# The moving matmul operands placed 64 bytes off the stationary ones, modulo 128

## The chip, the core and the metric

The kernel runs on one core of one Trainium2 chip, as one program in one launch. The metric is the device time of that launch in microseconds, as the median of the runs shown. One further execution is profiled; the times of single instructions come from that one.

## What is computed

Two trunk layers of a diffusion backbone on 256 latent tokens of width 2048 (batch 1), with all weights in float32. Cut to what matters:

```python
for i in range(2):                       # layer 0: pooling mixer, layer 1: gated MLP
    shift_x, scale_x, gate_x = split(silu(c) @ ada_w[i] + ada_b[i], 3)
    hx = rms_norm(x, norm_g[i]) * (1 + scale_x) + shift_x
    if i == 0:
        z, g = split(hx @ w_in, 2)       # 2048 -> 2 x 4096
        y = pool_mix(z, w_grp) * scale   # centred window means, then 4 maps 1024 -> 1024
        yx = (y * silu(g)) @ w_out       # 4096 -> 2048
    else:
        z = hx @ w_in                    # 2048 -> 3 x 4096
        u, v = split(gelu(z[:, :8192]), 2)
        v = layer_norm(v, ln_g, ln_b)
        s = w_s . v + b_s                # per 128 positions, 8 head groups
        yx = (u * s * silu(z[:, 8192:])) @ w_out
    x = x + gate_x * yx
```

The context stream of the reference never reaches the output here, and the kernel leaves it out.

## The kernel before

Every large product is `[256 tokens, K] @ [K, 512 columns]`, one block of 512 output columns at a time, for two halves of 128 tokens. One step along K of a block is a unit: 128 rows of K by 512 columns of weight. A float32 product is made of three matmuls in the type float32r (one pass each): both operands are split into a high part and a low rest, and `hi*hi + hi*lo + lo*hi` is summed in PSUM.

In these matmuls the activations are the stationary operand (`lhsT`, 128x128, put into the array by a weight load of its own, which the profile shows as PEld LDWEIGHTS), and the weights are the moving one (`rhs`, 128x512, 2048 bytes in each partition). The stationary tiles are `hh` and `hl` (the normalised input, high and low), `q` (the pooled rows) and `big` (the gated branch before the output product). The moving ones are `whi` and `wlo`. Line 621 multiplies `whi` by the high part, line 622 `wlo` by the high part, line 623 `whi` by the low part. Each matmul has a weight load, since neighbours differ in the stationary operand as recorded.

Weights come from HBM in 1 MB tiles (`raw`, ring of four, queue of SP). Line 98 (ScalarE) copies half a tile into `whi`, rounded to float32r, and line 99 (VectorE) writes the rest into `wlo`, each with three buffers; that is two units. `split_step` runs `LOOK` = 2 such pairs ahead of the matmuls. Between the weights the same ring carries the 96 tiles of `ada_w`, which VectorE multiplies by `silu(c)` and sums (line 245).

Some smaller matmuls use other tiles: line 322 has `big` stationary and the band matrix `bnd` (tag `cst`, 128x256) moving; lines 489 to 491 have the spatial weights (tag `cst`) stationary and `big` or `gs` moving; line 280 transposes through an identity.

SBUF tiles come from pools, and a pool lays its tags one behind the other in the order in which they are first asked for. Pool `sb` (opened first) holds all large tiles, `small` the constants. All sizes in `sb` are multiples of 2048 bytes, and the pool begins at byte 16512 of each partition, which is 129 x 128. So every large tile begins at a multiple of 128.

Of the kernel before, what the change touches and what calls it, by code (L numbers as in the profile page):

```python
# [27 lines left out]
RING = 4  # L28
LOOK = 2
LEAD = (0, 1)  # L30

# [41 lines left out]
def backbone(ctx: ExitStack, tc, x, c, ng, adab, ada, w, pscale, band, invcnt, lng, lnb, wsT, bs, out):  # L75
    nc = tc.nc
    sb = ctx.enter_context(tc.tile_pool(name="sb", bufs=1))
    small = ctx.enter_context(tc.tile_pool(name="small", bufs=1))
    pp = ctx.enter_context(tc.tile_pool(name="pp", bufs=1, space=bass.MemoryType.PSUM))

    uid = [0]

    def st(shape, dt, tag, bufs):
        uid[0] += 1
        return sb.tile(shape, dt, tag=tag, name=f"{tag}_{uid[0]}", bufs=bufs)

    def const(shape, name, dt=F32):
        return small.tile(shape, dt, tag=name, name=name, bufs=1)

    def big(shape, dt):  # L90
        return st(shape, dt, "big", 16)
# [23 lines left out]
    for s, v in enumerate(EARLY):  # L115
        u = sum(e - f for _, f, e in v)
        n1 = 2 * CHUNK[s + 2]
        for j in range(n0, n1):
            while load < begin + u * (j + 1 - n0) / (n1 - n0) / 4 - LEAD[min(s, len(LEAD) - 1)]:
                order.append(("w", load))  # L120
# [22 lines left out]
    def ring_load():  # L143
        e = ring_at[0]
        if e >= len(order):
            return
        ring_at[0] += 1
        kind, i = order[e]
        t = st([P, 2048], F32, "raw", RING)
        src = w[i] if kind == "w" else ada[i]  # L150
        parts = 2 if i < 2 else 1
        for q in range(parts):
            s = slice(q * 2048 // parts, (q + 1) * 2048 // parts)
            nc.sync.dma_start(out=t[:, s], in_=src[:, s])
        ring_tile[e] = t


    c_row = st([P, D], F32, "raw", RING)[0:1, :]
    nc.sync.dma_start(out=c_row, in_=c)
    xin = {}  # L160
# [4 lines left out]
    for _ in range(RING):  # L165
        ring_load()

    ng_sb = const([P, 2, KD], "ng_sb")
    nc.scalar.dma_start(out=ng_sb, in_=ng)
    ab_sb = const([P, 2, 3, KD], "ab_sb")  # L170
    nc.scalar.dma_start(out=ab_sb, in_=adab)
    ident = const([P, P], "ident")
    make_identity(nc, ident)
    ones = const([P, P], "ones")
# [6 lines left out]
    icnt = const([P, NT, NG], "icnt")  # L181
    bs_sb = const([P, 8], "bs_sb")
# [27 lines left out]
    sq0 = const([P, NT, 2], "sq0")  # L210
# [3 lines left out]
    nrm = const([P, 4, NT], "nrm")  # L214
# [191 lines left out]
    sq1 = const([P, NT, 4], "sq1")  # L406
# [194 lines left out]
    for i in range(nsteps):  # L601
# [5 lines left out]
        for u in range(2):  # L607
            n = 2 * i + u
            blk, k = units[n]
            last = n in breaks or k + 1 == blk.nk  # L610
# [109 lines left out]
```

## Time and the profile before

| | |
|---|---|
| three runs | 1403.9, 1407.91, 1408.12 us |
| median | 1407.91 us |
| profiled execution | 1404.94 us, its span from first to last instruction 1403.1 us |
| TensorE busy | 1379.0 us, 98% of the span |
| VectorE busy | 1010.9 us, 72% |
| ScalarE busy | 672.5 us, 48% |
| granted TensorE clock, mean | 0.998 of full |
| HBM | 362.38 MB read, 260 GB/s over the span |

The profiled execution lies 2.97 us below the median and within the range of the three runs. TensorE's busy share counts overlapping matmuls once, so 98% says that the engine had work in flight nearly always. It does not say how fast that work went.

### The profile page before, as it was taken

How to read it: one execution, taken by the hardware profiler on the slowest of the kernel's cores; microseconds unless marked ns; L12 is line 12 of the kernel's file. 1: busy time of each engine (PE TensorE's matmuls, PEld its weight loads, DVE VectorE, ACT ScalarE, POOL GpSimd, SP SyncE). 2: the span in 40 equal slices, each digit the busy share in tenths (PEclk: the TensorE clock that was granted, in tenths of full speed). 3: DMA queues.
4: the chain of work that ended last, by engine and by line, in shares of the span. 5: the costliest groups of instructions: out<-in, count | busy, mean ns of one | idle time of the engine just before them, and what ended most of it. 6: DMA issues, size and time to landing. Idle time of an engine off the chain costs nothing.

```text
span 1403.1 us, 16096 instructions
## 1 busy us (share of the span) xinstructions
PE 1379.0 (98%) x6192; PEld 1136.1 (81%) x6192; DVE 1010.9 (72%) x1305; ACT 672.5 (48%) x792; POOL 0.7 (0%) x6
## 2 busy tenths in 40 slices
PE   6899999999999999999999999999999999999998
PEld 4688887888888888888788888888888888888887
DVE  5899989998998788875765667976665555555553
ACT  8444434554554444444654445545545454544332
POOL 0000000000000000000000000000000000000000
PEclk9999999999999999999999999999999999999999
DMA  8898879878688898896466667776565545556561
GB/s 330 349 337 335 332 295 336 323 300 304 246 325 308 314 352 340 304 347 226 142 264 235 251 222 280 275 257 248 212 243 194 184 180 180 182 186 217 197 214 54
DMA packets 55663, 365.53 MB, mean 261 GB/s; under 512 B 6817, under 2 KB 6817, under 8 KB 13089
## 3 DMA queue, kind: packets, MB, share of 16 engines
q1 hardware_dynamic: 55298, 364.44, 70.2%
q8 instruction: 48, 0.79, 0.2%
q14 instruction: 29, 0.24, 0.0%
q10 hardware_dynamic: 288, 0.07, 0.0%
HBM read 362.38 MB, written 2.10 MB: 260 GB/s over the span
## 4 chain that ended last, share of the span: by engine, by line
PE 91%; DVE 5%; DMA 2%; ACT 1%; issue 1%; SPq 0%; ACTq 0%; DVEq 0%
PE mm L622 29%; PE mm L621 29%; PE mm L623 29%; DVE wlo L99 2%; DVE raw L245 2%; DMA raw<-in_w_dram 1%; PE aux L280 1%; PE aux L322 1%; ACT whi L98 1%; DMA raw<-in_ada_dram 1%; DVE big L628 0%; PE aux L489 0%; PE aux L491 0%; PE aux L490 0%; PE aux L402 0%
## 5 line engine op out<-in xcount | busy, mean ns | idle before, releaser
L99 DVE TENSOR_TENSOR wlo<-raw,whi 128x1024 fp32r<-128x1024 f32 x480 | 585.0, 1223 | 330.3 <-ACT whi L98 328.3
L98 ACT CAST whi<-raw 128x1024 fp32r<-128x1024 f32 x480 | 504.8, 1054 | 655.2 <-PE mm L623 603.1
L621 PE MATMUL mm<-whi,hh 128*128 128x512 f32 x1280 | 497.8, 391 | 4.5 <-ACT whi L98 2.4
L622 PE MATMUL mm<-wlo,hh 128*128 128x512 f32 x1280 | 500.3, 391 | 1.3 <-DVE wlo L99 1.2
L623 PE MATMUL mm<-whi,hl 128*128 128x512 f32 x1280 | 498.7, 390 | 0.0
L621 PEld LDWEIGHTS mm<-whi,hh 128*128 128x128 f32 x1280 | 240.2, 188 | 56.1 <-ACT whi L98 3.9
L622 PEld LDWEIGHTS mm<-wlo,hh 128*128 128x128 f32 x1280 | 240.8, 188 | 53.8 <-DVE wlo L99 4.3
L623 PEld LDWEIGHTS mm<-whi,hl 128*128 128x128 f32 x1280 | 240.7, 188 | 50.1 <-DVE hl L274 0.6
L245 DVE SCALAR_TENSOR_TENSOR raw<-raw,sc 128x1024 f32<-128x1024 f32 x192 | 229.4, 1220 | 17.9 <-DMA raw<-in_ada_dram 17.8
L622 PE MATMUL mm<-wlo,big 128*128 128x512 f32 x512 | 199.3, 389 | 0.0
L623 PE MATMUL mm<-whi,big 128*128 128x512 f32 x512 | 199.2, 389 | 0.0
L621 PE MATMUL mm<-whi,big 128*128 128x512 f32 x512 | 199.2, 389 | 0.0
L622 PEld LDWEIGHTS mm<-wlo,big 128*128 128x128 f32 x512 | 96.1, 188 | 20.3 <-DVE wlo L99 0.4
L623 PEld LDWEIGHTS mm<-whi,big 128*128 128x128 f32 x512 | 96.1, 188 | 19.9
L621 PEld LDWEIGHTS mm<-whi,big 128*128 128x128 f32 x512 | 96.1, 188 | 19.8
L621 PE MATMUL mm<-whi,q 128*128 128x512 f32 x128 | 50.1, 392 | 0.0
L623 PE MATMUL mm<-whi,q 128*128 128x512 f32 x128 | 49.8, 389 | 0.0
L622 PE MATMUL mm<-wlo,q 128*128 128x512 f32 x128 | 49.8, 389 | 0.0
L628 DVE TENSOR_TENSOR big<-mm,big 128x512 f32<-128x512 f32 x52 | 34.0, 684 | 0.4 <-PE mm L623 0.4
L623 PEld LDWEIGHTS mm<-whi,q 128*128 128x128 f32 x128 | 24.0, 188 | 5.0
L622 PEld LDWEIGHTS mm<-wlo,q 128*128 128x128 f32 x128 | 24.0, 188 | 4.9
L621 PEld LDWEIGHTS mm<-whi,q 128*128 128x128 f32 x128 | 24.0, 188 | 4.9
(105 smaller groups left out, 543.7 us busy)
## 6 DMA issues: line engine op xcount, KB each, us to landing
raw<-in_w_dram SPq DMA_DIRECT2D x238, 1024.0 KB, 5.0
raw<-in_ada_dram SPq DMA_DIRECT2D x94, 1024.0 KB, 5.7
big<-in_x_dram SPq DMA_DIRECT2D x4, 512.0 KB, 6.0
raw<-in_ada_dram SPq DMA_DIRECT2D x4, 512.0 KB, 9.0
raw<-in_w_dram SPq DMA_DIRECT2D x4, 512.0 KB, 10.3
q<-in_x_dram SPq DMA_DIRECT2D x8, 256.0 KB, 6.8
gate<-in_lng_dram SPq DMA_DIRECT2D x8, 256.0 KB, 5.0
gate<-in_lnb_dram SPq DMA_DIRECT2D x8, 256.0 KB, 4.3
```

Source lines behind the costliest of these rows:

```text
L98: nc.scalar.copy(hi, src)
L99: nc.vector.tensor_tensor(out=lo, in0=src, in1=hi.bitcast(F32), op=ALU.subtract)
L245: nc.vector.scalar_tensor_tensor(t[:, s], t[:, s], 1.0, sc[:, s], op0=ALU.mult, op1=ALU.mult, accum_out=dots[:, lay, what, k, half:half + 1])
L280: nc.tensor.transpose(tp[:, k - k0, tk * P:(tk + 1) * P], src(k, tk), ident)
L322: nc.tensor.matmul(o, lhsT=z[:, tk, ct * P:(ct + 1) * P], rhs=bnd[:, g, tk, :], start=(n == 0), stop=(n == 3))
L621: nc.tensor.matmul(blk.ps[tk], lhsT=lh, rhs=rh, start=(new and v == u), stop=False)
L622: nc.tensor.matmul(blk.ps[tk], lhsT=lh, rhs=rl, start=False, stop=False)
L623: nc.tensor.matmul(blk.ps[tk], lhsT=ll, rhs=rh, start=False, stop=end)
L628: nc.vector.tensor_tensor(out=blk.part[tk], in0=ps[tk], in1=blk.part[tk], op=ALU.add)
```

## The change

Tiles with the tags `whi`, `wlo` and `cst` come from a pool of their own, `moving`, opened behind `small`. Five small constants go to a fourth pool, `last`, behind it, so that `small` then ends 64 bytes past a multiple of 128.

```diff
+MOVING = ("whi", "wlo", "cst")
+LAST = ("icnt", "bs_sb", "nrm", "sq0", "sq1")
...
     sb = ctx.enter_context(tc.tile_pool(name="sb", bufs=1))
     small = ctx.enter_context(tc.tile_pool(name="small", bufs=1))
+    moving = ctx.enter_context(tc.tile_pool(name="moving", bufs=1))
+    last = ctx.enter_context(tc.tile_pool(name="last", bufs=1))
...
     def st(shape, dt, tag, bufs):
         uid[0] += 1
-        return sb.tile(shape, dt, tag=tag, name=f"{tag}_{uid[0]}", bufs=bufs)
+        pool = moving if tag in MOVING else sb
+        return pool.tile(shape, dt, tag=tag, name=f"{tag}_{uid[0]}", bufs=bufs)
 
     def const(shape, name, dt=F32):
-        return small.tile(shape, dt, tag=name, name=name, bufs=1)
+        pool = last if name in LAST else small
+        return pool.tile(shape, dt, tag=name, name=name, bufs=1)
```

What the two built programs say of the first byte of each tag's first buffer, and of its rest modulo 128 (further buffers follow at 2048, 4096 or 8192 bytes):

```
tag          before: byte, mod 128     changed: byte, mod 128
raw          16512   0                 16512   0
big          49280   0                 49280   0
cst          114816  0                 196416  64
sc           123008  0                 114816  0
hh           131200  0                 123008  0
hl           147584  0                 139392  0
whi          168064  0                 204608  64
wlo          180352  0                 216896  64
q            192640  0                 159872  0
gs, t, gate          0                         0
```

The instructions of every engine, their order and the semaphores that they wait for are the same in both programs, row by row; only addresses and line numbers differ.

## Rows read from the trace of the kernel before

**Rows 1.** The page: span, engines, granted clock, and the chain that ended last.

```profile
span 1403.1 us, 16096 instructions
...
PE 1379.0 (98%) x6192; PEld 1136.1 (81%) x6192; DVE 1010.9 (72%) x1305; ACT 672.5 (48%) x792; POOL 0.7 (0%) x6
...
PE mm L622 29%; PE mm L621 29%; PE mm L623 29%; DVE wlo L99 2%; DVE raw L245 2%; DMA raw<-in_w_dram 1%; PE aux L280 1%; PE aux L322 1%; ACT whi L98 1%; DMA raw<-in_ada_dram 1%; DVE big L628 0%; PE aux L489 0%; PE aux L491 0%; PE aux L490 0%; PE aux L402 0%
```

**Rows 2.** Costliest groups: count | busy us, mean ns | idle before, releaser.

```profile
L99 DVE TENSOR_TENSOR wlo<-raw,whi 128x1024 fp32r<-128x1024 f32 x480 | 585.0, 1223 | 330.3 <-ACT whi L98 328.3
...
L622 PE MATMUL mm<-wlo,hh 128*128 128x512 f32 x1280 | 500.3, 391 | 1.3 <-DVE wlo L99 1.2
...
L622 PE MATMUL mm<-wlo,big 128*128 128x512 f32 x512 | 199.3, 389 | 0.0
...
L622 PE MATMUL mm<-wlo,q 128*128 128x512 f32 x128 | 49.8, 389 | 0.0
L628 DVE TENSOR_TENSOR big<-mm,big 128x512 f32<-128x512 f32 x52 | 34.0, 684 | 0.4 <-PE mm L623 0.4
```

**Rows 3.** Stretches: PE, PEld, DVE, ACT, POOL busy us; clock, DMA share, GB/s.

```profile
45.50:48.30 2.80, 2.80 (x8) 2.19 (x7) 2.80 (x4) 0.11 (x1) 0.00 (x0) 0.50 0.99 410
50.00:200.00 150.00, 148.15 (x657) 120.58 (x656) 134.37 (x192) 68.78 (x79) 0.00 (x0) 1.00 0.87 326
200.00:400.00 200.00, 199.43 (x936) 165.76 (x935) 182.91 (x263) 101.20 (x130) 0.00 (x0) 1.00 0.82 306
400.00:600.00 200.00, 200.00 (x913) 166.27 (x913) 166.58 (x222) 90.75 (x111) 0.00 (x0) 1.00 0.85 323
606.00:645.00 39.00, 39.00 (x174) 32.31 (x173) 29.94 (x43) 18.41 (x22) 0.00 (x0) 1.00 0.82 304
1000.00:1200.00 200.00, 200.00 (x900) 165.89 (x899) 112.80 (x117) 103.20 (x117) 0.00 (x0) 1.00 0.56 199
```

**Rows 4.** Timeline of PE, 606 to 645: start us, us; first and last of 174.

```profile
605.71 0.39 PE L623 MATMUL mm<-whi,big 128*128 128x512 f32 x1
...
644.92 0.39 PE L623 MATMUL mm<-whi,big 128*128 128x512 f32 x1
```

**Rows 5.** Timeline of PE, 44 to 48.3, clock at half: start us, us.

```profile
45.82 0.63 PE L622 MATMUL mm<-wlo,hh 128*128 128x512 f32 x1
...
47.95 0.63 PE L622 MATMUL mm<-wlo,hh 128*128 128x512 f32 x1
```

**Rows 6.** Timeline of PE from 252.7, line 322's and those behind it.

```profile
252.76 2.08 PE L322 MATMUL aux<-cst,big 128*128 128x256 f32 x16
254.68 0.40 PE L621 MATMUL mm<-whi,hh 128*128 128x512 f32 x1
...
255.84 0.39 PE L623 MATMUL mm<-whi,hl 128*128 128x512 f32 x1
256.06 0.39 PE L621 MATMUL mm<-whi,hh 128*128 128x512 f32 x1
...
257.88 0.39 PE L623 MATMUL mm<-whi,hl 128*128 128x512 f32 x1
```

**Rows 7.** Groups of PE, 120 to 140: count | busy us, mean ns | idle.

```profile
L623 PE MATMUL mm<-whi,hl 128*128 128x512 f32 x30 | 11.7, 389 | 0.0
```

**Rows 8.** Weight loads from 671.6: start us, us [idle before, releaser].

```profile
671.67 0.19 PEld L623 LDWEIGHTS mm<-whi,big 128*128 128x128 f32 x1
673.77 0.19 PEld L287 LDWEIGHTS mm<-q,ones 128*128 128x128 f32 x1 [1.91 <-DVE q L415]
```

**Rows 9.** Groups of PE, 671.85 to 672.2, the matmul that starts at 671.89.

```profile
L623 PE MATMUL mm<-whi,big 128*128 128x512 f32 x1 | 0.4, 388 | 0.0
```

**Rows 10.** Weight loads from 677.9.

```profile
679.03 0.19 PEld L622 LDWEIGHTS mm<-wlo,hh 128*128 128x128 f32 x1
679.63 0.19 PEld L623 LDWEIGHTS mm<-whi,hl 128*128 128x128 f32 x1 [0.41 <-DVE hl L274]
```

**Rows 11.** Groups of PE, 679.28 to 679.45; line 622's starts at 679.26.

```profile
L621 PE MATMUL mm<-whi,hh 128*128 128x512 f32 x1 | 0.4, 397 | 0.0
L622 PE MATMUL mm<-wlo,hh 128*128 128x512 f32 x1 | 0.4, 397 | 0.0
```

## Prediction

> **What bounds the kernel now.** I read the page first. TensorE is busy for 1379.0 of 1403.1 us, and the chain that ended last goes through the three matmul lines 621 to 623 for 87% of the span [rows 1]. By stage it is the same: from 200 to 600 us and from 1000 to 1200 TensorE has work in flight for all but 0.57 of 600 us [rows 3]. What differs between stages is how close the others are. In 200 to 400 us VectorE is busy for 182.91 of 200 us and HBM delivers 306 GB/s; in 1000 to 1200 us it is 112.80 us and 199 GB/s. So a faster TensorE gains all of it in the second half of the program, and less in the first. VectorE's and ScalarE's work on `whi` and `wlo` runs ahead of the matmuls: line 99 waited 328.3 us for ScalarE's line 98 [rows 2].
>
> The next view is the pace of the matmuls, start to start, not their listed length of 389 to 391 ns, which overlaps the next one. From 605.71 to 644.92 us lie 173 steps, all of 512 columns: 39.21 / 173 = 226.6 ns [rows 4], at a granted clock of 1.00 [rows 3]. At 2.4 GHz 512 columns are 213.3 ns. So each matmul takes 13.3 ns, or 32 cycles, more than its columns. At half the clock (0.50 granted in the stretch [rows 3]), from 45.82 to 47.95 us, five steps take 2.13 us, 426 ns each, and 512 columns at 1.2 GHz are 426.7 ns: nothing is lost there [rows 5]. The loss is therefore no fixed number of array cycles; something that feeds the array doesn't keep up with 2.4 GHz. There are (1280 + 512 + 128) x 3 = 5760 such matmuls on lines 621 to 623 [rows 2], as lines 621 and 623 have the same counts. What is lost is 5760 x 13.3 ns = 77 us of the span. That is the only place where this change can find much.
>
> **The change part by part.** No instruction, order or wait is added, removed or moved; DMA transfers keep their sizes and their queue. There is thus nothing to count but addresses. `whi`, `wlo` and `cst` now begin 64 bytes past a multiple of 128, and the stationary tiles stay on multiples of it. Before, all of them began on one, so the trace has no matmul whose two operands differ in this. Its effect has to be bounded.
>
> First the matmuls. If moving reads and weight loads disturbed each other through their addresses, the loss would have to be there while both run, and be gone when a matmul streams with no weight load beside it. The trace has such matmuls: the last ones ahead of an idle time. The matmul that starts at 671.89 us has its own weights loaded from 671.67, and the next load begins at 673.77 [rows 8]. It lasts 388 ns [rows 9]; those with a load beside them last 389 ns [rows 7]. The listed length moves with the pace (below), so without the 13.3 ns I would expect some 376 ns. About 1 ns is missing, not 13. I take that 1 ns as what two streams cost each other in the settled state: 5760 x 1 ns = 6 us at the very most, and my value is nothing.
>
> A second reading points the same way. The pace isn't always 226.6. Behind each change of kind, line 322's for instance, it is slower for a few matmuls: from 254.68 to 255.84 us five steps take 1.16 us, 232 ns each, and from 256.06 to 257.88 eight take 1.82 us, 227.5 ns [rows 6]. So some state of TensorE decides, and settles. In such a disturbed state, too, there is one matmul that streams alone: that of line 622 at 679.26 us, whose successor's weights are not asked for until 679.63 [rows 10]. It lasts 397 ns, as long as the one ahead of it, which had a load beside it [rows 11]. The 9 ns of that state are kept with no second reader. Both levels of loss belong to the moving stream by itself, as far as these rows go.
>
> One row speaks against that. Line 322's matmuls have 256 columns, and 16 of them start in 254.68 - 252.76 = 1.92 us [rows 6], 120 ns each: 13.3 ns above 106.7, the same loss for half the columns. A loss of the moving stream alone would be half as large. A loss per weight load would look like this. I give it less weight, because a weight load there has only 120 ns, and 0.19 us is its listed length [rows 8], so it may be the loads that set that pace.
>
> Then the other engines. Line 99 reads `raw` and `whi` and writes `wlo`, so its operands too now lie on different rests. It takes 1223 ns for 1024 columns against 684 ns for 512 of line 628, which reads one operand from PSUM [rows 2]: 1.05 ns a column. One VectorE column can't be split further by these rows, and no excess stands out that a shifted address could remove: I take 0, with the bounds 5% either way, 480 x 61 ns = 29 us of VectorE's time, nearly all of it hidden behind TensorE except in 200 to 400 us. Line 98 has more slack still: ScalarE is busy for 101.20 of 200 us there. The five constants in `last` are used by short instructions; I cost them at nothing.
>
> The sum is therefore 0 us on a profiled execution of 1404.94 us. The median of the runs is 2.97 us above that one, and I forecast the median: 1407 us.
>
> The Trainium skill, in SBUF - State Buffer (Who interferes with whom), gives TensorE two read ports of its own, one for the moving operand and one for weight loads, and says that it never waits on anyone. The 388 ns agree with that; the 120 ns of line 322 and the changing pace are not explained by it. By that rule the sum is 0 too, and both rivals below would fall away.
>
> **Rivals.** *The two streams do collide, and the offset parts them (faster).* For it speak line 322's row, the pace that depends on a state, and that the loss is gone at the lower clock. Against it speak the two matmuls that stream alone. The most it could give is the whole 77 us. From 600 us on, TensorE's matmuls fill the time with the others at ease: 803 us hold 3540 of them at 226.6 ns, of which I put some 3390 to lines 621 to 623, worth 45 us. The 2370 before that are worth 32 us, but VectorE with 182.91 of 200 us would have no slack left when TensorE's 200 us become 189, and HBM would have to go from 306 to 324 GB/s; I take half, 16 us. All of it gives 1407 - 61 = 1346 us, half of the loss 1376; I name 1358 us as its middle.
>
> In TensorE: Matmul & The Clock Gate (Back-to-back issue gap), the Trainium skill has N / 2.4 + 2.5 ns, 215.8 ns for 512 columns, measured on 2-byte operands. The trace does not agree for these 4-byte ones, with 226.6 ns. If the offset brought this kernel to that figure, the estimate would be 5760 x 10.8 ns = 62 us less.
>
> *The offset moves the settled state to a slower one.* The state behind a change of kind costs 232 - 226.6 = 5.4 ns a matmul [rows 6]. Before the change it lasts for some five matmuls, and with other starting addresses it could be the one that stays. If it does, 5760 x 5.4 ns = 31 us are added, since nothing else hides TensorE's time: 1438 us. It decides as soon as a seventh of the matmuls stay there (4.2 us). Half of them give 1422 us. For it speaks only that such states exist; against it, that all of them ended in the same pace, whichever buffers of `whi`, `wlo`, `hh` and `big` were in use.
>
> *The change doesn't do what it says:* excluded, since the built program places the tiles as described.
>
> **How the numbers follow.** No change has 0.47, faster 0.38 (line 322's row, and a loss of 77 us whose cause I can't name), slower 0.15. A measurement of this kernel tells about 0.3% from no change, 4.2 us, which is also the spread of the three runs. The likeliest case gives 1407 us, with 1402 to 1412 as its own range. For 8 in 10 the range must reach into both others: down to 1350, which leaves out the nearly full gain (about 0.08), and up to 1422, half of the slower case (about 0.07).
>
> **What would show it.** Right: in the changed trace the pace in a stretch of 512-column matmuls is again 226 to 227 ns, line 322's 16 take 1.92 us, the matmul ahead of an idle time lasts 388 ns, and VectorE's line 99 takes 1223 ns. The first rival shows as a pace between 214 and 222 ns, with TensorE's idle time growing in 200 to 400 us, where line 621 would wait for ScalarE and VectorE. The second shows as a pace of 230 to 236 ns in long stretches. The prediction is wrong if the moving stream's own loss depends on where it begins within 128 bytes; nothing in the trace could tell me that, as all begin on the same rest.

## The result, and the profile after

| | before | changed |
|---|---|---|
| median of the runs | 1407.31 us (4 runs, 1403.9 to 1408.12) | 1440.06 us (4 runs, 1438.93 to 1440.28) |
| profiled execution's span | 1403.1 us | 1438.1 us |
| ratio | | 1.0236, 95% interval 1.0218 to 1.0254 |

The change makes the kernel 33 us slower. The forecast was 1407 us with a range of 1350 to 1422: it missed, and on the side that had 0.15.

The page and the stretches of the changed kernel, which answer to [rows 1] to [rows 3] (its lines 627 to 629 are 621 to 623 of before, 105 is 99, 328 is 322):

```profile
span 1438.1 us, 16096 instructions
...
PE 1415.2 (98%) x6192; PEld 1137.0 (79%) x6192; DVE 1013.6 (70%) x1305; ACT 670.9 (47%) x792; POOL 0.7 (0%) x6
...
L105 DVE TENSOR_TENSOR wlo<-raw,whi 128x1024 fp32r<-128x1024 f32 x480 | 585.8, 1223 | 369.7 <-ACT whi L104 367.1
...
L628 PE MATMUL mm<-wlo,big 128*128 128x512 f32 x512 | 202.2, 395 | 0.0
```

```profile
200.00:400.00 200.00, 200.00 (x923) 163.48 (x923) 181.78 (x258) 100.11 (x128) 0.00 (x0) 1.00 0.80 302
400.00:600.00 200.00, 200.00 (x891) 162.16 (x891) 160.73 (x213) 88.59 (x109) 0.00 (x0) 1.00 0.84 314
...
1000.00:1200.00 200.00, 200.00 (x876) 161.31 (x875) 111.55 (x118) 97.51 (x109) 0.00 (x0) 1.00 0.56 199
```

TensorE is as busy as before and at the full clock, but gets through less: 876 matmuls in 1000 to 1200 us where there were 900. VectorE's line 105 takes the same 1223 ns, and its engine only waits longer. So the other engines' work takes as long as before, and the pace of the matmuls has changed. The timeline of PE shows it; of 151 matmuls the first and the last:

```profile
624.80 0.39 PE L629 MATMUL mm<-whi,big 128*128 128x512 f32 x1
...
659.80 0.40 PE L629 MATMUL mm<-whi,big 128*128 128x512 f32 x1
```

That is 35.00 us in 150 steps, 233.3 ns each, where [rows 4] gave 226.6. Over the whole trace, the mean of all steps of under 260 ns between neighbouring 512-column matmuls is 226.92 ns before (5722 steps) and 233.31 ns after (5734). 5760 x 6.39 ns = 36.8 us. The span grew by 35.0 us, so some 2 us came back elsewhere; the steps of over 260 ns, which hold waits, sum to 34.0 us before (72 steps) and 29.4 us after (60). Above each kernel's own pace that is 17.7 and 15.4 us, about those 2 us.

Two more places of the timeline. Line 328's sixteen 256-column matmuls, whose moving operand moved too, became faster, 266.66 - 264.84 = 1.82 us against 1.92 in [rows 6]:

```profile
264.84 1.98 PE L328 MATMUL aux<-cst,big 128*128 128x256 f32 x16
266.66 0.39 PE L627 MATMUL mm<-whi,hh 128*128 128x512 f32 x1
```

And the matmul that starts at 686.85 us, with no weight load beside its stream (the next load comes at 688.64), lasts 397 ns, where [rows 9] had 388:

```profile
L629 PE MATMUL mm<-whi,big 128*128 128x512 f32 x1 | 0.4, 397 | 0.0
L628 PE MATMUL mm<-wlo,big 128*128 128x512 f32 x1 | 0.4, 394 | 0.0
```

### The profile page after: what moved, and what is told of

It is laid out like the page before. It is cut to its first block, busy times and chain, and to the rows that moved or that the text cites. A ratio compares the mean times of both kernels' runs of the same rounds, so it can differ in the third digit from the quotient of the medians.

```text
span 1438.1 us, 16096 instructions
## 1 busy us (share of the span) xinstructions
PE 1415.2 (98%) x6192; PEld 1137.0 (79%) x6192; DVE 1013.6 (70%) x1305; ACT 670.9 (47%) x792; POOL 0.7 (0%) x6
## 4 chain that ended last, share of the span: by engine, by line
PE 96%; DVE 2%; ACT 1%; DMA 1%; issue 0%; SPq 0%; DVEq 0%; ACTq 0%
PE mm L628 31%; PE mm L627 31%; PE mm L629 31%; PE aux L286 2%; PE aux L328 1%; DVE raw L251 1%; DMA raw<-in_ada_dram 1%; ACT whi L104 1%; DVE wlo L105 0%; PE aux L495 0%; PE aux L496 0%; PE aux L408 0%; PE aux L497 0%; PE mm L293 0%; ACT big L643 0%
## 5 line engine op out<-in xcount | busy, mean ns | idle before, releaser
L105 DVE TENSOR_TENSOR wlo<-raw,whi 128x1024 fp32r<-128x1024 f32 x480 | 585.8, 1223 | 369.7 <-ACT whi L104 367.1
L627 PE MATMUL mm<-whi,hh 128*128 128x512 f32 x1280 | 505.2, 397 | 4.3 <-ACT whi L104 2.3
L628 PE MATMUL mm<-wlo,hh 128*128 128x512 f32 x1280 | 507.2, 396 | 0.5 <-DVE wlo L105 0.5
L629 PE MATMUL mm<-whi,hl 128*128 128x512 f32 x1280 | 505.5, 395 | 0.0
L628 PE MATMUL mm<-wlo,big 128*128 128x512 f32 x512 | 202.2, 395 | 0.0
L629 PE MATMUL mm<-whi,big 128*128 128x512 f32 x512 | 202.1, 395 | 0.0
L627 PE MATMUL mm<-whi,big 128*128 128x512 f32 x512 | 202.1, 395 | 0.0
```

Of the source, the lines that this page charges most:

```text
L105: nc.vector.tensor_tensor(out=lo, in0=src, in1=hi.bitcast(F32), op=ALU.subtract)
L627: nc.tensor.matmul(blk.ps[tk], lhsT=lh, rhs=rh, start=(new and v == u), stop=False)
L628: nc.tensor.matmul(blk.ps[tk], lhsT=lh, rhs=rl, start=False, stop=False)
L629: nc.tensor.matmul(blk.ps[tk], lhsT=ll, rhs=rh, start=False, stop=end)
```

## Experiments

The theory after the result (R): what counts is the distance between the moving and the stationary operand, modulo some power of two; the moved tiles took a distance with a slower settled pace. Its rivals: the moving operand's own start counts (A), or the other engines' traffic does, or the pool itself.

### The matmuls by themselves, one distance after the other

A program of its own, without any of the reference's work:

```python
def burst(name, n, pick):
    ps = bank(name)
    for i in range(n):
        s, m = pick(i)
        nc.tensor.matmul(ps, lhsT=sta[:, s:s + 128], rhs=mov[:, m:m + CB], start=(i == 0), stop=(i == n - 1))
    return ps
...
for d in range(0, 65):
    burst(f"m{4 * d}b", N, lambda i: (0, d))
for s in (8, 16, 24, 32, 64):
    burst(f"s{4 * s}b", N, lambda i: (s, 0))
burst("both64b", N, lambda i: (16, 16))
...
```

Here and below, `mov` and `sta` begin at distance 0 modulo 256; the number in a burst's name is what is added, in bytes.

> The matmuls by themselves: nothing else runs, and the computation of the reference is left out. Bursts of 32 float32r matmuls (128x128 stationary, 128x512 moving), one burst for each distance of the moving operand from the stationary one in steps of 4 bytes from 0 to 256, then some with the stationary operand moved instead, with both moved, and with operands that alternate. Theory R (what counts is the distance of the two operands modulo some power of two): 226.7 ns a matmul at 0 and 233.3 at 64, a pattern that repeats after 128 or 256 bytes, the burst with both at 64 at 226.7. Theory A (what counts is where the moving operand itself begins): both at 64 gives 233.3, and the stationary one moved alone gives 226.7. Rival (neither; the other engines' reads and writes in the full kernel make the difference): 226.7 or less at every distance.

The timeline of PE in this program: start us, length us, name, count. A matmul's listed length is 0.16 us more than its pace, so the pace of a burst is (length - 0.16) / 32, its first matmuls included.

```profile
18.92 7.42 PE L42 MATMUL m0b<-mov,sta 128*128 128x512 f32 x32
...
70.94 7.42 PE L42 MATMUL m28b<-mov,sta 128*128 128x512 f32 x32
...
137.65 7.48 PE L42 MATMUL m64b<-mov,sta 128*128 128x512 f32 x32
...
204.58 7.83 PE L42 MATMUL m100b<-mov,sta 128*128 128x512 f32 x32
...
256.98 7.62 PE L42 MATMUL m128b<-mov,sta 128*128 128x512 f32 x32
...
376.49 7.63 PE L42 MATMUL m192b<-mov,sta 128*128 128x512 f32 x32
...
495.85 7.43 PE L42 MATMUL m256b<-mov,sta 128*128 128x512 f32 x32
...
510.58 7.63 PE L42 MATMUL s64b<-mov,sta 128*128 128x512 f32 x32
...
525.53 7.58 PE L42 MATMUL s128b<-mov,sta 128*128 128x512 f32 x32
...
540.21 7.46 PE L42 MATMUL both64b<-mov,sta 128*128 128x512 f32 x32
```

Nothing else runs, and distances still make the pace. The means of the 19 settled steps of each burst: 226.6 ns at 0, 228.7 at 64, 233.5 at 128, 233.2 at 192, 226.6 at 256; at 4 bytes it is 236.6, at 100 it is 240.0. With both operands 64 further it is 226.7 again, and with the stationary one 64 further (192 the other way) 233.5. So theory R holds, A falls, and the other engines are not needed. The pattern repeats after 256 bytes, not after 128; with the stationary operand 1024 bytes further the pace is 226.6 too. Where one operand alternates between two starts 64 bytes apart, it is 230.2 (stationary) and 230.4 (moving). No distance is faster than 0; eight others of the 65 bursts equal it (28, 60, 108, 156, 236, 240, 252 and 256).

One distance doesn't always give one pace, though. At 128 it is 233.5 ns with the moving operand moved and 231.9 with the stationary one (`s128b`), and at 100 the second program of bursts (below) settles at 235.5, not at 240.0. Bursts repeated at 0, 32, 64, 96, 160, 192 and 224 agree within 0.4 ns.

That sets the change right: "64 modulo 128" isn't one case. In the changed kernel `whi` begins at byte 204608 and `hh` at 123008; their distance is 192 modulo 256, and the burst at 192 has 233.2 ns, the kernel 233.3.

### The full kernel with other distances

All large tiles 64 bytes further, by the order in which pools are opened:

```diff
-    sb = ctx.enter_context(tc.tile_pool(name="sb", bufs=1))
     small = ctx.enter_context(tc.tile_pool(name="small", bufs=1))
-    moving = ctx.enter_context(tc.tile_pool(name="moving", bufs=1))
+    sb = ctx.enter_context(tc.tile_pool(name="sb", bufs=1))
+    moving = sb
```

> All large tiles, moving and stationary, begin 64 bytes past a multiple of 128. Theory R (distance of the two): the pace is 226.7 ns again and the time that of before, 1407 us. Theory A (the moving operand's own start): 233.3 ns and 1440 us.

The other five change one line of the changed kernel each, and by it where the pool `moving` begins (`off32`, `off96`, `pool0`, `off64t`, `off128` in this order):

```diff
-LAST = ("icnt", "bs_sb", "nrm", "sq0", "sq1")
+LAST = ("icnt", "bs_sb", "nrm", "sq0", "sq1", "mv")
+LAST = ("bs_sb", "nrm", "sq0", "sq1")
+LAST = ("nrm", "sq0", "sq1")
+LAST = ("icnt", "bs_sb", "nrm", "sq0", "sq1", "psc")
+LAST = ("icnt", "bs_sb", "nrm", "sq0", "sq1", "gv", "mv")
```

> The moving tiles 32 bytes off the stationary ones instead of 64. Theory R with a period of 64: a pace other than at 0 and at 64, between 214 and 236 ns, so 1345 to 1460 us; if only bit 6 of the address counted, it would be 226.7 ns and 1407 us.

> The moving tiles 96 bytes off. Theory R: a pace of its own, 214 to 236 ns (1345 to 1460 us); if only bit 6 counted, 233.3 ns and 1440 us.

> The changed kernel with two of the five constants put back into the pool small, so that the moving tiles lie at distance 0 modulo 256 from the stationary ones, in their own pool. By the burst at distance 0 (226.6 ns): the time of before, 1407 us, within 0.3%. A rival by which the own pool costs something: still 1440.

> The moving tiles 64 bytes past the stationary ones modulo 256; in the changed kernel it is 192 modulo 256, which is also 64 modulo 128. If distances repeat after 256 bytes, the burst at 64 (228.7 ns against 226.6) gives 5760 x 2.1 ns = 12 us more, 1418 us. If they repeat after 128 bytes, it is the changed kernel again, 1440 us.

> The moving tiles 128 bytes past the stationary ones modulo 256. If distances repeat after 256 bytes, the burst at 128 (233.5 ns) gives 5760 x 6.9 ns = 40 us more, 1446 us. If they repeat after 128 bytes, it is distance 0 and 1407 us.

The burst's pace is that of the first sweep, the kernel's the mean of all steps under 260 ns in its own trace. The two names with 32 and 96 are at 160 and 224 modulo 256.

| kernel | distance mod 256 | burst, ns | kernel, ns | median us | ratio to before, 95% interval |
|---|---|---|---|---|---|
| `pool0` | 0 | 226.6 | 226.9 | 1406.51 | 1.0006 (0.9994 to 1.0018) |
| `all64` | 0 | 226.7 | 227.0 | 1407.08 | 1.0007 (0.9997 to 1.0017) |
| `off64t` | 64 | 228.7 | 229.3 | 1417.17 | 1.0081 (1.0063 to 1.0100) |
| `off128` | 128 | 233.5 | 232.6 | 1435.16 | 1.0207 (1.0192 to 1.0223) |
| `off96` | 224 | 233.4 | 233.3 | 1439.49 | 1.0242 (1.0220 to 1.0263) |
| changed kernel | 192 | 233.2 | 233.3 | 1440.06 | 1.0236 (1.0218 to 1.0254) |
| `off32` | 160 | 234.3 | 234.2 | 1444.27 | 1.0274 (1.0254 to 1.0293) |

The pool of its own costs nothing (`pool0`), nor do starts at 64 with no distance (`all64`). The time goes with the distance. `off32` also excludes that bit 6 of the address alone counts (1407 us expected, 1444 measured); `off96` by itself would not, as 1440 was expected by that rule and 1439 came. `off64t` settles the period: 1417 us as the burst said, not 1440. `off128` was expected at 1446 and came out at 1435. Its pace is 0.9 ns under the burst's, which is 5 us, and some waits shrink as in the changed kernel; why this one settles otherwise than in the burst I don't know, but at 128 the two bursts differ as well (233.5 and 231.9).

### What the loss belongs to

A second program of bursts cuts the operands, takes 2-byte ones, and has single matmuls with waits on both sides.

```python
for m in (0, 16, 25, 48):
    for c in (128, 96, 64, 32):
        burst(f"m{4 * m}c{c}w512b", N, m=m, c=c)
...
for m in (0, 16, 32, 64, 96):
    burst(f"bfm{2 * m}b", N, m=m, bf=True)
for m in (0, 8, 16, 25, 33, 48, 0, 25):
    barrier(burst("keep", 24))
    barrier(burst(f"single{4 * m}b", 1, m=m))
```

> The matmuls by themselves again, the rest of the computation left out. Bursts of 32 with the stationary operand cut to 96, 64 and 32 columns, with the moving one cut to 384, 320 and 256, with 2-byte operands, and single matmuls with idle time on both sides. Theory L (the weight load of the next matmul takes reads from the moving stream, and the distance of the two decides how many): the loss above the moving columns falls with the stationary columns, from 13.3 ns at 128 to about 7 at 64 and 3 at 32 at distance 0, and from 20 and 27 in proportion at 192 and 100; a single matmul, whose stream has no load beside it, lasts the same at every distance. Theory M (the moving stream loses by itself): the loss stays at 13.3 ns however few stationary columns there are, is halved with 256 moving columns, and a single matmul shows the same differences between distances as the bursts, up to 13 ns between 0 and 100.

Its timeline of PE; names have the distance, the stationary columns (c) and the moving ones (w):

```profile
18.62 7.42 PE L48 MATMUL m0c128w512b<-mov,sta 128*128 128x512 f32 x32
...
40.60 7.57 PE L48 MATMUL m0c32w512b<-mov,sta 128*32 128x512 f32 x32
...
77.55 7.70 PE L48 MATMUL m100c128w512b<-mov,sta 128*128 128x512 f32 x32
...
107.88 7.62 PE L48 MATMUL m192c128w512b<-mov,sta 128*128 128x512 f32 x32
...
137.50 5.73 PE L48 MATMUL m0c128w384b<-mov,sta 128*128 128x384 f32 x32
...
147.76 4.00 PE L48 MATMUL m0c128w256b<-mov,sta 128*128 128x256 f32 x32
...
162.13 4.03 PE L48 MATMUL m100c128w256b<-mov,sta 128*128 128x256 f32 x32
...
176.24 3.80 PE L48 MATMUL m192c128w256b<-mov,sta 128*128 128x256 f32 x32
...
193.71 7.07 PE L48 MATMUL bfm64b<-movb,stab 128*128 128x512 bf16 x32
...
220.42 0.50 PE L48 MATMUL single0b<-mov,sta 128*128 128x512 f32 x1 [0.33 <-DVE mov L52]
...
247.47 0.50 PE L48 MATMUL single132b<-mov,sta 128*128 128x512 f32 x1 [0.26 <-DVE mov L52]
```

Both theories fall as they were stated. A quarter of the weight load (32 columns) doesn't reduce the loss at distance 0: the settled pace is 231.6 ns against 226.7. Nor is the loss there halved with half the moving columns: it is 13.3 ns with 512 (226.68), 384 (173.32), 320 (146.68) and 256 (120.00), as if it were paid once a matmul.

At the other distances it does change with the widths. With 512, 384, 320 and 256 moving columns it is 19.9, 13.3, 13.3 and 6.7 ns at 192, and 22.2, 20.0, 15.9 and 14.3 ns at 100. With 32 stationary columns, 0, 64 and 192 all settle at 231.6 ns, and 100 at 236.7. So what the distance adds is no fixed price for a matmul.

With 2-byte operands the loss is 2.5 ns at each of the five distances tried (215.8 ns). A single matmul shows no order by distance: 503 and 502 ns at 0, 503 at 32, 494 at 64, 502 and 492 at 100, 502 at 132, 505 at 192, while bursts differ between 0 and 100 by 13 ns in the first sweep and by 9 in this one. Two at the same distance are up to 10 ns apart, so eight of them exclude such a difference but not a small one. As far as they show, the distance acts where one matmul follows another.

Every matmul of this program has a weight load of its own (1204 and 1204), though the stationary operand is the same all through a burst. So a load needs no change of the stationary operand, and the reason given for the kernel's loads ahead of the prediction falls: its lines 621 and 622 share their stationary tile.

### Is there a faster combination?

Bursts in the kernel's order of three: high weights by high part, low by high, high by low, with a distance for each of the three tiles against the fourth, all 512 combinations in steps of 32 bytes, in two programs.

```python
burst(f"a{32 * a}b{32 * b}d{32 * d}x", 30,
      lambda i: ((0, 0, 8 * d)[i % 3], (8 * a, 8 * b, 8 * a)[i % 3]))
```

> The matmuls by themselves, the rest left out. First bursts with 512 down to 448 moving columns at distance 0. Theory S (settled matmuls lock to a grid of 16 cycles of 2.4 GHz, 6.67 ns, since 544, 560, 576, 416, 352, 288 and 272 cycles were the settled periods so far): the pace falls in steps of 6.67 ns and stays flat between them. Rival (a fixed 32 cycles for each matmul): it falls with every column, 0.42 ns each. Then bursts in the kernel's order of three (high by high, low by high, high by low), with the three kinds of tiles at all distances in steps of 32 bytes, the high weights at 0 to 96. Theory S: the sum of three settled matmuls is a multiple of 16 cycles, so the mean can be 224.4 ns (1616 cycles) if some combination allows it, else 226.7 or more. Rival (each matmul has its own price by its own distance, which the sweep of single distances gives): the mean of three is never below 226.6.

> The same bursts of three with the high weights at 128 to 224 bytes; the theories expect the same as for the first half.

The timeline of PE of the first program:

```profile
19.66 7.42 PE L42 MATMUL w512b<-mov,sta 128*128 128x512 f32 x32
...
34.20 7.41 PE L42 MATMUL w504b<-mov,sta 128*128 128x504 f32 x32
...
84.02 6.99 PE L42 MATMUL w472b<-mov,sta 128*128 128x472 f32 x32
...
104.02 6.96 PE L42 MATMUL a0b0d0x<-mov,sta 128*128 128x512 f32 x30
...
409.93 6.96 PE L42 MATMUL a0b160d128x<-mov,sta 128*128 128x512 f32 x30
```

No combination is below 226.67 ns; only two of the 512 reach it, those shown. The mean over all is 232.0 ns. The kernel before has its tiles at 0, 0, 0. So these programs point to no faster version, and none was run; steps finer than 32 bytes were not tried in threes.

On the grid of 16 cycles, the fixed 32 cycles fall: 504 columns take the same 226.68 ns as 512. But flat steps with sharp edges are not what the bursts show either (223.5 ns at 500, 223.3 at 496, 222.0 at 492, 225.8 at 488, 213.3 at 472). What held is that settled patterns add up to multiples of 16 cycles: 500 columns alternate between two lengths with a mean of 536 cycles, two of which are 67 x 16; the best triples behind those two, apart from one at 227.7 ns, take 3 x 228.87 ns, 1648 cycles or 103 x 16.

### One part of the change alone

```diff
-MOVING = ("whi", "wlo", "cst")
+MOVING = ("wlo",)
```

and the same with `("whi",)`.

> Only the low parts of the weights moved (192 past the stationary tiles modulo 256), the high parts and the band matrix where they were. By the burst of three with these distances (228.9 ns against 226.7): 5760 x 2.2 = 13 us more, 1419 us. Rival (each matmul has its own price by its own distance): a third of the whole change's loss, 11 us, 1417 us; the two differ little here.

> Only the high parts moved. By the burst of three with these distances (234.65 ns): 5760 x 8.0 = 46 us more, 1451 us at most (a few us may come back from waits that shrink, as in the changed kernel, 1447), slower than the whole change. Rival (own price by own distance): two thirds of the whole change's loss, 22 us, 1428 us.

`wlo_only`: 1417.76 us, ratio 1.0086 (1.0071 to 1.0101). `whi_only`: 1445.44 us, 1.0285 (1.0268 to 1.0302), slower than both together. Prices of single matmuls that add up are excluded: the parts cost 12 and 39 us, the whole 33. The timeline of `whi_only` shows it too:

```profile
629.94 0.40 PE L628 MATMUL mm<-wlo,big 128*128 128x512 f32 x1
630.18 0.40 PE L629 MATMUL mm<-whi,big 128*128 128x512 f32 x1
630.41 0.40 PE L627 MATMUL mm<-whi,big 128*128 128x512 f32 x1
630.65 0.40 PE L628 MATMUL mm<-wlo,big 128*128 128x512 f32 x1
```

The matmul on line 628, whose tiles didn't move, is followed after 240 ns; over the whole trace the step behind it is 237.5 ns, the longest of the three lines (235.4 and 230.1 behind the other two). What a matmul pays depends on its neighbours' distances.

## Why the prediction was wrong

**The bound was read right.** The pace of the matmuls, 226.6 ns against 213.3, was named as the one place where addresses could act, and only it changed. Line 99's 0 was right (1223 ns again), and so was the order of instructions, which is the same.

**The step that failed** is "I take that 1 ns as what two streams cost each other in the settled state [...] and my value is nothing." It came from matmuls that stream with no weight load beside them and last as long as the others, 388 and 397 ns. The rows were right, but the conclusion was not. They show that a matmul's listed length stays when the next load doesn't come; they don't show that the operands' distance is without effect. In place of nothing the runs have 6.39 ns a matmul for the change, 36.8 us, and they have it from the operands' distance and from the matmuls around. The changed kernel repeats the pattern on the new level: 397 ns alone, 394 beside it. So the length of a matmul that streams alone can't tell whether the distance counts. That such a matmul has paid its loss before the next load is due would fit this, but no run shows when it is paid.

**Line 322's row was underrated.** It gave 13.3 ns at 256 columns as at 512, and the prediction set it aside as the loads' own limit. The second program shows the same 13.3 ns at 320 and 384 columns, at the distance that the row has, and at distance 192 the same 256 columns take only 113.4 ns, so the loads don't set that pace. The row was the better witness: the distance acts on it too, though the other way.

**The rival that came true** is the second, "the offset moves the settled state to a slower one", at 1438 us; measured 1440.06. Its price was 5.4 ns a matmul and turned out as 6.39. That 1438 came so close is partly luck: the price was that of a passing state at distance 0, which no run shows to be the state that stays at 192; other distances gave 1417 to 1444 us, and some 2 us came back from waits. Its chance of 0.15 rested on the argument that the states all ended in one pace, whichever buffers were used. Those buffers were all at distance 0 modulo 256, so they were one sample and not many. With the bursts in hand, most distances are slower than 0: of the eight that 32-byte steps allow, seven.

**The last warning was half right**: the trace could not tell what an unseen distance does. It named the moving stream's own start as the danger, and `all64` shows that this is without effect.

**The first rival**, the streams collide and the offset parts them, is excluded as a gain at 512 columns: no distance of the sweep is below 226.6 ns, and neither is any of the 512 combinations. Only line 328's 256-column matmuls gained, 1.82 us for 1.92.

**Two rules beside the runs.** The rule of the Trainium skill in SBUF - State Buffer (Who interferes with whom), that TensorE's two read ports, one for the moving operand and one for weight loads, are independent, doesn't account for these traces: the distance of its two operands costs up to 13.4 ns a matmul (240.0 against 226.6). That TensorE never waits on anyone, by the same section, is not touched: with no other engine at work the burst at 192 has 233.2 ns, and the kernel 233.3. The figure of the Trainium skill in TensorE: Matmul & The Clock Gate (Back-to-back issue gap), N / 2.4 + 2.5 ns and so 215.8 ns for 512 columns, which it gives for an isolated matmul and with no type, agrees with the 2-byte bursts, 215.8 ns, and doesn't carry over to 4-byte ones, where no distance reached it.

What stays open: which pair of reads it is that the distance acts on, a matmul's with its own weights', with the next matmul's weights', or through the order in which they are started; and why the settled patterns fit 16 cycles. Shown are only the period of 256 bytes at the distances tried, the sums of 16 cycles, that neighbours in a sequence change it, and that 2-byte operands don't have it at the five distances tried.

## What to carry to other kernels

For float32r matmuls, lay the moving and the stationary tiles on the same rest modulo 256 bytes: here, with 512 moving columns, no other of 512 layouts was faster, and the seven others that ran in the full kernel cost 0.8 to 2.9%. Before a layout is changed, run bursts of the matmuls alone at the distances in question; they gave the pace of the full kernel within 1 ns. Run each distance more than once: at 100 bytes two bursts settled 4.5 ns apart. And a pace that many buffers share is one sample if all of them have the same address bits; it says nothing about others.

## What the runs showed of the hardware

- The pace of float32r matmuls depends on the operands' distance in steps as fine as 4 bytes: 226.6 ns at 0, 236.6 at 4, 226.6 at 28, 240.0 at 100 (235.5 in the second program).
- At distance 0 the loss is 13.3 ns with 256, 320, 384 and 512 moving columns, 15.1 to 22.5 ns at the eleven widths from 448 to 508 that were tried, and not smaller with 32 stationary columns (18.3 ns). With 2-byte operands it is 2.5 ns at all five distances tried.
- At 256 columns distance 192 is faster than 0, 113.4 against 120.0 ns, and at 512 columns it is slower; what is best for one width is not for another.
- At half the clock nothing is lost before or after (steps of 425 to 428 ns, as listed; 512 columns at 1.2 GHz are 426.7).
